# A two-layer encoder in split float32: fourteen more seven-product pairs, weight parts in idle task pages, a new arrangement of the block sums

## The chip, the cores and the metric

The kernel runs on one core of a Trainium2 chip. The metric is the device time of one execution in microseconds. Three runs of the kernel before gave 2572.28, 2573.15 and 2574.47 us; the median is 2573.15 us. The engines are TensorE (PE, with its weight loads shown apart as PEld), VectorE (DVE), ScalarE (ACT), GpSimd (POOL) and SyncE (SP).

## The reference

Two layers over 256 rows of width 4096. Each layer normalises the rows, multiplies by a 4096 x 11264 matrix, runs grouped-query attention and a two-way retention on the parts, gates both, and multiplies by a 4096 x 4096 matrix. All is float32.

```python
for l in range(DEPTH):
    h = rmsnorm(x, norm_w[l])
    proj = h @ w_in[l]                                   # 4096 -> 11264
    aq, ak, av, ag, rq, rk, rv, rg = jnp.split(proj, SPLIT_POINTS, axis=-1)
    aq = apply_axial_rope(rmsnorm(aq), rope) * attn_scale
    ak = apply_axial_rope(rmsnorm(ak), rope)
    a_out = jax.nn.silu(ag) * gqa_attention(aq, ak, av)
    r = bidirectional_retention(rope(rq), rope(rk) * ret_scale, rv, log_gf, log_gb)
    r_out = jax.nn.silu(rg) * rmsnorm(r, ret_norm[l])
    x = x + jnp.concatenate([a_out, r_out], axis=-1) @ w_out[l]   # 4096 -> 4096
return rmsnorm(x, final_norm)
```

## The kernel before

**Products.** The time goes to the two projections. A float32 operand is held as two parts, a high one (rounded to the type fp32r by a copy on ACT) and a low one (the rest, by a subtraction on DVE), and one product is three matmuls of 128x512: high by high, high by low, low by high. The work is cut into 30 blocks of 1024 output columns: phase 0 and 2 (the input projections of the layers) have 11 blocks each, phase 1 and 3 (the output projections) 4 each. A block is written (phase, block), as (1, 2). A block sums over 16 pairs of 256 rows of the inner dimension. A pair is a 2x2 by 2x2 product of submatrices. An "eight" does it with eight products; a "seven" does it with seven products of sums of submatrices (Strassen), so it needs three matmuls fewer, but ready-made sums of the activations (`x7h`, `x7l`: seven forms) and sums of the weights (`wsum`), which DVE makes. Even pairs are always sevens, odd pairs eights, whose activations (`x8h`, `x8l`) hold six forms. The table `MORE` turns an odd pair into a seven in some blocks; `add_forms` then makes the lacking forms from the eight's ones and keeps them in the tile `more` (lines 2000 to 2030).

**Weights.** The weights of an eight come as two raw pages of 128x1024 (kinds A and B). Each gets a high part (`whi`, ACT) and a low part (`wlo`, DVE); a "far" page gets its low part from ACT and a DMA that adds the raw weights to it (`fhi`, `flo`). A seven has four pages: A (raw), T and U (the sums `wsum`, one of 1024 elements and two halves of 512, the second made from the first), and B, of which half is used (`whb`, `wlb`, 512). The buffers: 6 raws, 4 highs, 3 lows, 2 sums, 2 fars, 1 half. Class `Slots` (line 581) counts them.

**Sums of a block.** Each block fills seven PSUM banks M1 to M7. When a bank is done, `combining` (line 1801) adds it to the result tiles `ca` and `cb` on DVE; the next block can only start in a bank that has been read. M5 is added twice, once to each half of `cb`.

**Other work.** Tasks (attention, retention, rotary, gates, residuals) run beside the projections and use 8 task pages of 128x1024 (`PAGES`).

**What sets the order.** The order on every engine is written out while the program is built: clocks of the engines and of the DMA queues are kept in Python, and at each step the engine whose clock is earliest takes the most urgent piece that its model says is ready (`pick`, line 966). `WAYS` gives knobs by block: how early high parts ("high"), sums ("sums") and activations ("split") are made, when tasks may come first ("rush"), and how far ahead of the next block's need the M sums are due ("wait"). On the chip each engine then goes through its list in that order and waits at semaphores; PE too, whose list mixes the products of the tasks into those of the block.

Of the kernel before, what the change touches and what calls it, by code (L numbers as in the profile page):

```python
# [52 lines left out]
WAY = {"rush": 2.8, "split": 6.0, "high": 3.2, "sums": (2.0, 1.99, 1.98), "wait": None}  # L53
WAYS = {
    (0, 1): {"rush": 4.2, "split": 6.0, "high": 3.2, "sums": (2.0, 1.99, 1.98), "wait": 0},
    (0, 2): {"rush": 2.8, "split": 6.0, "high": 3.2, "sums": (2.0, 0.5, 0.4), "wait": None},
    (0, 3): {"rush": 2.4, "split": 6.0, "high": 3.2, "sums": (2.0, 1.99, 1.98), "wait": 0.5},
    (0, 4): {"rush": 2.4, "split": 6.0, "high": 3.2, "sums": (2.0, 1.99, 1.98), "wait": 1},
    (0, 5): {"rush": 2.8, "split": 6.0, "high": 3.2, "sums": (2.0, 1.99, 1.98), "wait": 1},
    (0, 10): {"rush": 2.8, "split": 6.0, "high": 4.5, "sums": (2.0, 1.99, 1.98), "wait": None},  # L60
    (1, 0): {"rush": 2.8, "split": 6.0, "high": 3.2, "sums": (2.0, 1.99, 1.98), "wait": 1},
    (2, 3): {"rush": 4.2, "split": 6.0, "high": 3.2, "sums": (2.0, 1.99, 1.98), "wait": None},
    (2, 4): {"rush": 2.0, "split": 6.0, "high": 3.2, "sums": (2.0, 1.99, 1.98), "wait": 1},
    (2, 5): {"rush": 2.8, "split": 6.0, "high": 3.2, "sums": (2.0, 1.99, 1.98), "wait": 1},
    (2, 10): {"rush": 2.8, "split": 6.0, "high": 4.5, "sums": (2.0, 1.99, 1.98), "wait": None},
    (3, 0): {"rush": 2.8, "split": 6.0, "high": 3.2, "sums": (2.0, 1.99, 1.98), "wait": 1},
# [60 lines left out]
def constants():  # L127
# [27 lines left out]
A11, A12, S4, A22N, S1, S2, S3 = range(7)  # L155
TWO_FORMS = {A11: 0, A12: 2, S3: 4}
# [2066 lines left out]
```

## Time and profile before

| | |
|---|---|
| median of three runs | 2573.15 us |
| the profiled execution | 2574.22 us |
| its span, first to last instruction | 2572.4 us |
| PE busy | 2552.3 us (99%), 11393 matmuls |
| DVE busy | 2405.6 us (94%), 3100 instructions |
| ACT busy | 1954.7 us (76%) |
| mean granted PE clock | 0.998 of full speed |

Busy times are unions: a row of 1.22 us may overlap the next. A matmul's row lasts longer than the distance to the next one, since they are pipelined.

### The profile page before, as it was taken

How to read it: one execution, taken by the hardware profiler on the slowest of the kernel's cores; microseconds unless marked ns; L12 is line 12 of the kernel's file. 1: busy time of each engine (PE TensorE's matmuls, PEld its weight loads, DVE VectorE, ACT ScalarE, POOL GpSimd, SP SyncE). 2: the span in 40 equal slices, each digit the busy share in tenths (PEclk: the TensorE clock that was granted, in tenths of full speed). 3: DMA queues.
4: the chain of work that ended last, by engine and by line, in shares of the span. 5: the costliest groups of instructions: out<-in, count | busy, mean ns of one | idle time of the engine just before them, and what ended most of it. 6: DMA issues, size and time to landing. Idle time of an engine off the chain costs nothing.

```text
span 2572.4 us, 34567 instructions
## 1 busy us (share of the span) xinstructions
PE 2552.3 (99%) x11393; PEld 2099.4 (82%) x11393; DVE 2405.6 (94%) x3100; ACT 1954.7 (76%) x2797; POOL 453.1 (18%) x591
## 2 busy tenths in 40 slices
PE   9999999999999999999999999999999999999998
PEld 5888888888888888788888888887888888888886
DVE  7999999999999999999999999999999989999887
ACT  8877777787777788767887776877887777787675
POOL 0012121221222120112111212211212221201010
PEclk9999999999999999999999999999999999999999
DMA  8989999998998998999999999989999998989897
GB/s 309 311 263 318 269 280 293 281 309 270 277 286 278 284 272 239 277 300 301 304 301 280 292 279 287 283 282 282 296 277 278 276 293 264 283 242 284 252 281 238
DMA packets 212533, 724.91 MB, mean 282 GB/s; under 512 B 25456, under 2 KB 32240, under 8 KB 212352
## 3 DMA queue, kind: packets, MB, share of 16 engines
q1 hardware_dynamic: 147616, 521.31, 57.4%
q0 software_dynamic: 64736, 201.40, 33.8%
q8 instruction: 89, 1.46, 0.2%
q14 instruction: 92, 0.75, 0.1%
HBM read 674.37 MB, written 48.23 MB: 281 GB/s over the span
## 4 chain that ended last, share of the span: by engine, by line
PE 92%; DVE 4%; issue 1%; DMA 1%; POOL 0%; ACT 0%; DVEq 0%; POOLq 0%; ACTq 0%
PE M L1280 89%; PE ps L1280 3%; DVE wlo L315 2%; DVE wsum L315 1%; DVE cb L315 1%; DVE ca L315 0%; DMA flo<-in_w_in 0%; POOL rst L574 0%; DMA nw<-in_norm_wT 0%; PE ps L1115 0%; DVE wlb L315 0%; DVE x8l L315 0%; DVE x7l L315 0%; DVE xf L315 0%; ACT whi L315 0%
## 5 line engine op out<-in xcount | busy, mean ns | idle before, releaser
L315 DVE TENSOR_TENSOR wlo<-wsum,whi 128x1024 fp32r<-128x1024 f32 x486 | 592.2, 1219 | 70.2 <-PE M L1280 54.5
L315 ACT CAST whi<-wsum 128x1024 fp32r<-128x1024 f32 x486 | 509.6, 1049 | 185.9 <-PE M L1280 93.9
L315 DVE TENSOR_TENSOR wlo<-wraw,whi 128x1024 fp32r<-128x1024 f32 x499 | 604.7, 1214 | 6.1 <-ACT whi L315 2.4
L315 ACT CAST whi<-wraw 128x1024 fp32r<-128x1024 f32 x499 | 514.7, 1044 | 94.0 <-PE M L1280 44.2
L1280 PE MATMUL M<-whi,x7h 128*128 128x512 f32 x1428 | 557.1, 390 | 0.3 <-DVE cb L315 0.3
L1280 PE MATMUL M<-whi,x7l 128*128 128x512 f32 x1428 | 555.9, 389 | 0.0
L1280 PE MATMUL M<-wlo,x7h 128*128 128x512 f32 x1428 | 442.7, 391 | 3.0 <-DVE wlo L315 2.8
L1280 PE MATMUL M<-whi,x8h 128*128 128x512 f32 x1026 | 400.1, 390 | 0.5 <-DVE ca L315 0.5
L1280 PE MATMUL M<-whi,x8l 128*128 128x512 f32 x1026 | 399.5, 389 | 0.0
L1280 PE MATMUL M<-fhi,x8h 128*128 128x512 f32 x832 | 324.0, 389 | 0.0
L1280 PE MATMUL M<-fhi,x8l 128*128 128x512 f32 x832 | 323.9, 389 | 0.0
L439 POOL DMA_DIRECT2D flo<-in_w_in x153 | 136.0, 889 | 1029.9 <-ACT flo L315 907.9
L1280 PEld LDWEIGHTS M<-wlo,x7h 128*128 128x128 f32 x1428 | 265.8, 188 | 61.6 <-DVE wlo L315 8.2
L1280 PEld LDWEIGHTS M<-whi,x7h 128*128 128x128 f32 x1428 | 268.2, 188 | 56.7 <-DVE cb L315 1.2
L1280 PEld LDWEIGHTS M<-whi,x7l 128*128 128x128 f32 x1428 | 268.2, 188 | 55.8 <-issue 0.5
L315 DVE TENSOR_TENSOR wsum<-wraw 128x1024 f32<-128x1024 f32 x243 | 296.0, 1218 | 7.7 <-DMA wraw<-in_w_in 3.8
L1280 PE MATMUL M<-wlo,x8h 128*128 128x512 f32 x1026 | 302.1, 390 | 0.4 <-DVE wlo L315 0.4
L315 ACT CAST fhi<-wraw 128x1024 fp32r<-128x1024 f32 (+1 forms) x210 | 218.8, 1042 | 107.0 <-PE M L1280 63.4
L1280 PE MATMUL M<-flo,x8h 128*128 128x512 f32 x832 | 228.4, 389 | 0.0
L1280 PEld LDWEIGHTS M<-whi,x8h 128*128 128x128 f32 x1026 | 192.6, 188 | 42.3 <-DVE ca L315 2.1
L1280 PEld LDWEIGHTS M<-wlo,x8h 128*128 128x128 f32 x1026 | 192.2, 188 | 41.9 <-DVE wlo L315 2.0
L315 ACT ACTIVATE flo<-fhi 128x1024 fp32r<-128x1024 f32 (+1 forms) x210 | 221.3, 1054 | 6.5
(268 smaller groups left out, 3527.3 us busy)
## 6 DMA issues: line engine op xcount, KB each, us to landing
wraw<-in_w_in SPq DMA_DIRECT2D x703, 512.0 KB, 5.9
wraw<-in_w_out SPq DMA_DIRECT2D x256, 512.0 KB, 6.0
flo<-in_w_in POOLq DMA_DIRECT2D x153, 512.0 KB, 8.6
flo<-in_w_out POOLq DMA_DIRECT2D x53, 512.0 KB, 8.5
full<-next_dram POOLq DMA_DIRECT2D x18, 512.0 KB, 9.8
p_dram<-room POOLq DMA_DIRECT2D x64, 128.0 KB, 5.1
pT<-p_dram POOLq DMA_DIRECT2D x16, 512.0 KB, 8.4
next_dram<-room POOLq DMA_DIRECT2D x40, 128.0 KB, 4.8
```

What stands on the lines that cost most here:

```text
L315: return call(out, *args, **kwargs)
L439: getattr(nc, name).dma_start(to, src, **kw)
L1280: nc.tensor.matmul(out, a, b, start=start, stop=stop)
```

## The change

The table `MORE` now names 14 pairs in 11 blocks instead of 5 pairs in 4 blocks. A list `groups_of` spreads the eights between the sevens. The fourth form is A22 instead of its negative, so that an eight's forms hold it already; `add_forms` makes three forms instead of four. The sums of a split, the rotary products, the query splits and the addition of M5 are done in one wide instruction each. `Slots` may take an idle task page for a high part, a low part or a weight sum (`lendable`), by knobs of the block. The knobs of all blocks are new, the order in which the last banks are finished is M3, M4, M5, M2, and `FARS` lists the far pages of nine blocks. The input tables, the first block's direct products, the final block's order and its tail are not in the diff.

```diff
-LAST_ORDER = ("M3", "M5", "M4", "M2")
+LAST_ORDER = ("M3", "M4", "M5", "M2")
-A11, A12, S4, A22N, S1, S2, S3 = range(7)
+A11, A12, A22, S4, S2, S1, S3, A21, D1 = range(9)
+FORMS = {"x7": (A11, A12, A22, S4, S2, S1, S3), "x8": (A11, A12, A21, A22, S3, D1)}
-NINE = ((0, 1), (2, 3), (4,), (6, 5), (7,), (8, 9), (10, 11), (12, 13), (14, 15))
-TEN = ((0, 1), (2,), (4, 3), (6,), (7, 5), (8,), (10, 9), (12,), (13, 11), (14, 15))
-MORE = {(1, 1): NINE, (1, 2): TEN,(3, 1): NINE, (3, 2): NINE}
+MORE = {
+    (0, 1): (9,), (0, 6): (13,), (0, 7): (11,),
+    (1, 1): (3, 11), (1, 2): (5, 13),
+    (2, 1): (5,), (2, 2): (7,), (2, 6): (7,), (2, 7): (5,),
+    (3, 1): (5, 13), (3, 2): (7,),
+}
-    (0, 3): {"rush": 2.4, "split": 6.0, "high": 3.2, "sums": (2.0, 1.99, 1.98), "wait": 0.5},
+    (0, 3): {"sums": (1.5, 0, -0.1), "lend": 1},
...
+    def lendable(n):
+        first = next((v for v in tasks if not v.begun and v.start()), None)
+        need = 0 if first is None else first.need - first.own + (0 if first.own else wanted[0])
+        need = max(need, 2 if to_border() < now_way("stop") else 0)
+        return held[0] + n + pledged() + need + spare() < PAGES and all(v() for v in idle[:n])
     class Slots:
         def ready(self):
-            return self.free and min(self.free) <= now.t
+            return (self.free and min(self.free) <= now.t) or (self.knob is not None and self.lent < now_way(self.knob) and lendable(self.pages))
...
+        def place_of(self, lent, name, n, dt):
+            if lent:
+                return sp.tile([P, 2, NB], dt, tag="pg", name=name, bufs=PAGES)
+            return t(wp, [P, 2, NB], name, n, dt)
...
         def end_u(self, g):
-            ve.tensor_sub(u[:, 1, :], u[:, 0, :], b[:, 1, :])
+            ve.tensor_sub(u[:, 1, :], b[:, 1, :], u[:, 0, :])
...
     def split_pair(p, v, phase, gains, across):
-            ve.tensor_sub(s1, a22n, x1[:, 0])
-            ve.tensor_sub(s3, x0[:, 0], x1[:, 0])
+            ve.tensor_sub(s13, s13, x1[:, 0:1].to_broadcast([P, 2, P // BLK, BLK]))
...
     def rotary(v, L, kind, to):
-            for h in range(2):
-                ve.tensor_mul(dsts[:, :, :, h, :], src[:, :, :, 1 - h, :], ...)
-            ve.tensor_mul(v4[:, m], v4[:, m], C[:, m, :].unsqueeze(1).to_broadcast([P, 4, HD]))
+        ve.tensor_mul(dst, src[:, :, :, :, ::-1, :], S.rearrange(...).unsqueeze(2).to_broadcast(wide))
+        ve.tensor_mul(v4, v4, C.unsqueeze(2).to_broadcast([P, MT, 4, HD]))
...
     def combining(acc, fin, c, order, pages=True):
-        ve.tensor_add(ca[:, 1, :], cb[:, 0, :], acc["M7"])
+        ve.tensor_add(cb[:, 1, :], cb[:, 0, :], acc["M7"])
             if b == "M5":
-                ve.tensor_add(cb[:, 1, :], ca[:, 1, :], acc["M5"])
-                ve.tensor_add(cb[:, 0, :], cb[:, 0, :], acc["M5"])
+                ve.tensor_add(cb, cb, acc["M5"].unsqueeze(1).to_broadcast([P, MT, NB]))
...
     def add_forms(p, phase):
-        ac.copy(parts[:, 0, 0], f[:, 4])
-        ac.copy(parts[:, 0, 2:4], f[:, 5:7])
-        ve.tensor_sub(parts[:, 1, 0], f[:, 4], f32(parts[:, 0, 0]))
-        ve.tensor_sub(parts[:, 1, 2:4], f[:, 5:7], f32(parts[:, 0, 2:4]))
+        ac.copy(parts[:, 0], f[:, 4:7])
+        ve.tensor_sub(parts[:, 1], f[:, 4:7], f32(parts[:, 0]))
```

**Place one: PE in block (0, 1), page A of pair 9.** The numbers tell tiles apart: `x8h_305` is pair 9's activations before, `x8h_315` after. Before, the page is an eight:

```order
L1280 MATMUL M3_978<-whi_1309,x8h_305 128x512
L1280 MATMUL M3_978<-whi_1309,x8l_306 128x512
L1280 MATMUL M5_994<-whi_1309,x8h_305 128x512
L1280 MATMUL M5_994<-whi_1309,x8l_306 128x512
L1280 MATMUL M4_999<-whi_1309,x8h_305 128x512
L1280 MATMUL M4_999<-whi_1309,x8l_306 128x512
L1280 MATMUL M2_1006<-whi_1309,x8h_305 128x512
L1280 MATMUL M2_1006<-whi_1309,x8l_306 128x512
L1280 MATMUL M3_978<-wlo_1345,x8h_305 128x512
L1280 MATMUL M5_994<-wlo_1345,x8h_305 128x512
L1280 MATMUL M4_999<-wlo_1345,x8h_305 128x512
L1280 MATMUL M2_1006<-wlo_1345,x8h_305 128x512
```

After, it is a seven's page A, with a form from `more`:

```order
L1378 MATMUL M1_964<-whi_1309,x8h_315 128x512
L1378 MATMUL M1_964<-whi_1309,x8l_316 128x512
L1378 MATMUL M3_970<-whi_1309,more_961 128x512 x2
L1378 MATMUL M1_964<-wlo_1321,x8h_315 128x512
L1378 MATMUL M3_970<-wlo_1321,more_961 128x512
```

Twelve matmuls into four banks have become six into two ("x2" is two rows that read alike); the seven's pages T, B and U follow further on, in all 21 matmuls against 24.

**Place two: DVE at the end of block (0, 3), where the banks are added to `ca` and `cb`.** Before:

```order
L315 TENSOR_TENSOR cb_3212<-ca_3211,M6_2580 128x512
L315 TENSOR_TENSOR wsum_3257<-wraw_3133,wsum_3241 128x512
L315 TENSOR_TENSOR ca_3211<-cb_3212,M7_2532 128x512
L315 TENSOR_TENSOR wsum_3257<-wsum_3257,wraw_3178 128x512
L315 TENSOR_TENSOR cb_3212<-cb_3212,M3_2488 128x512
L315 TENSOR_TENSOR cb_3212<-ca_3211,M5_2504 128x512
L315 TENSOR_TENSOR cb_3212<-cb_3212,M5_2504 128x512
L315 TENSOR_TENSOR wlo_3285<-wraw_3133,whi_3229 128x1024
L315 TENSOR_TENSOR ca_3211<-ca_3211,M4_2507 128x512
L315 TENSOR_TENSOR wlo_3309<-wraw_3190,whi_3249 128x1024
L315 TENSOR_TENSOR ca_3211<-ca_3211,M2_2512 128x512
```

After:

```order
L358 TENSOR_TENSOR cb_3189<-ca_3188,M6_2562 128x512
L358 TENSOR_TENSOR cb_3189<-cb_3189,M7_2524 128x512
L358 TENSOR_TENSOR cb_3189<-cb_3189,M3_2485 128x512
L358 TENSOR_TENSOR pTl_3227<-pT_3116,pTh_3226 128x1024
L358 TENSOR_TENSOR ca_3188<-cb_3189,M4_2504 128x512
L358 TENSOR_TENSOR cb_3189<-cb_3189,M5_2499 128x1024
L358 TENSOR_TENSOR wsum_3265<-wraw_3123,wsum_3214 128x512
L358 TENSOR_TENSOR wlo_3271<-wraw_3123,whi_3206 128x1024
L358 TENSOR_TENSOR sgT_3114<-ps_3255,sgT_3114 128x2x8x32
L358 TENSOR_TENSOR wsum_3265<-wraw_3152,wsum_3265 128x512
L358 TENSOR_TENSOR ca_3188<-ca_3188,M2_2509 128x512
```

M5's two additions of 512 are one of 1024 and come behind M4's; a low part of an attention task (`pTl`) and the product with the gate (`sgT`) now stand among them. The first `wlo` is the seventh row behind M6's in both; two of the six rows between are of 1024 elements after, none before.

**Place three: DVE in block (1, 1), where the added forms of the block's sevens are made.** Before, one set (pair 7), with two low parts at its end:

```order
L315 TENSOR_TENSOR forms_9872<-x8h_9082,x8l_9083 128x256 x2
L315 SCALAR_TENSOR_TENSOR forms_9872<-forms_9872 128x128
L315 TENSOR_TENSOR forms_9872<-forms_9872 128x128 x2
L315 TENSOR_TENSOR wlb_10064<-wraw_9913,whb_10054 128x512
L315 TENSOR_TENSOR wlo_10070<-wsum_10025,whi_10058 128x1024
L315 TENSOR_TENSOR wlo_10080<-wraw_9969,whi_10066 128x1024
L315 TENSOR_TENSOR wsum_10090<-wraw_9969,wsum_10039 128x512
L315 TENSOR_TENSOR wlo_10097<-wraw_9994,whi_10082 128x1024
L315 TENSOR_TENSOR wsum_10090<-wsum_10090,wraw_9976 128x512
L315 TENSOR_TENSOR wlo_10113<-wsum_10039,whi_10092 128x1024
L315 TENSOR_TENSOR more_9871<-forms_9872,more_9871 128x128
L315 TENSOR_TENSOR more_9871<-forms_9872,more_9871 128x256
```

After, the first of the two sets that the block now holds (pairs 3 and 11):

```order
L358 TENSOR_TENSOR forms_9851<-x8h_8840,x8l_8841 128x256 x2
L358 SCALAR_TENSOR_TENSOR forms_9851<-forms_9851 128x128
L358 TENSOR_TENSOR forms_9851<-forms_9851 128x128 x2
L358 TENSOR_TENSOR wlo_9981<-wsum_9927,whi_9950 128x1024
L358 TENSOR_TENSOR wlo_9989<-wraw_9869,whi_9960 128x1024
L358 TENSOR_TENSOR more_9850<-forms_9851,more_9850 128x384
L358 TENSOR_TENSOR wsum_9999<-wraw_9869,wsum_9954 128x512
L358 TENSOR_TENSOR wlo_10005<-wraw_9888,whi_9973 128x1024
```

The low parts of a set are one instruction of 384 elements; a second set, of the same instructions, stands 33 rows further down, ahead of the addition of the block's M6.

## Rows read from the trace of the kernel before

**Rows 1.** The page: span, and busy time, share and instructions of each engine.

```profile
span 2572.4 us, 34567 instructions
...
PE 2552.3 (99%) x11393; PEld 2099.4 (82%) x11393; DVE 2405.6 (94%) x3100; ACT 1954.7 (76%) x2797; POOL 453.1 (18%) x591
```

**Rows 2.** Windows: busy time (and instructions) of each engine, PE clock, DMA share, GB/s.

```profile
core 0: us, PE busy (x) PEld busy (x) DVE busy (x) ACT busy (x) POOL busy (x), PEclk, DMA share, GB/s
0.00:100.00 100.00, 96.51 (x352) 66.11 (x353) 86.17 (x149) 81.71 (x150) 5.21 (x10) 0.98 0.90 305
100.00:2500.00 2400.00, 2394.99 (x10776) 1983.52 (x10775) 2261.96 (x2876) 1830.62 (x2580) 439.06 (x570) 1.00 0.92 282
2500.00:2573.00 73.00, 60.77 (x268) 49.76 (x266) 57.44 (x77) 42.33 (x69) 8.87 (x11) 0.94 0.75 242
```

**Rows 3.** Waits of PE: what waited for what, us in total, times, longest.

```profile
PE M L1280 <- DVE wlo L315: 3.2, 10, 0.5
PE M L1280 <- ACT full L315: 1.9, 1, 1.9
PE ps L2160 <- DVE whi L2157: 1.5, 1, 1.5
PE ps L1280 <- DVE pTl L315: 0.8, 1, 0.8
```

**Rows 4.** Chain of waits, one unbroken run of matmuls: start, us, what.

```profile
710.37 48.30 PE M L1280 x213
```

**Rows 5.** Timeline of PE at 349: start, us, instruction [idle before <- releaser].

```profile
348.83 0.39 PE L1280 MATMUL M<-whi,x7l 128*128 128x512 f32 x1
349.74 0.73 PE L1280 MATMUL M<-wlo,x7h 128*128 128x512 f32 x2 [0.52 <-DVE wlo L315]
```

**Rows 6.** Timeline of PE at 1791, among the products of an attention task.

```profile
1790.36 0.40 PE L1280 MATMUL ps<-pTh,kv 128*128 128x512 f32 x1
1791.55 0.51 PE L1280 MATMUL ps<-pTl,kv 128*128 128x512 f32 x1 [0.80 <-DVE pTl L315]
```

**Rows 7.** Lines of DVE by form: count | busy us, mean ns | idle before.

```profile
L315 DVE TENSOR_TENSOR wlo<-wraw,whi 128x1024 fp32r<-128x1024 f32 x495 | 601.9, 1218 | 6.1 <-ACT whi L315 2.4 <-issue 1.1 <-ACT xf L315 0.9
L315 DVE TENSOR_TENSOR wlo<-wsum,whi 128x1024 fp32r<-128x1024 f32 x486 | 592.2, 1219 | 70.2 <-PE M L1280 54.5 <-ACT whi L315 13.2 <-ACT whb L315 1.4
L315 DVE TENSOR_TENSOR wsum<-wraw 128x1024 f32<-128x1024 f32 x243 | 296.0, 1218 | 7.7 <-DMA wraw<-in_w_in 3.8 <-DMA wraw<-in_w_out 2.7
...
L315 DVE TENSOR_TENSOR wsum<-wraw,wsum 128x512 f32<-128x512 f32 x243 | 166.2, 684 | 0.4
L315 DVE TENSOR_TENSOR wlb<-wraw,whb 128x512 fp32r<-128x512 f32 x243 | 165.5, 681 | 35.6 <-ACT whb L315 35.6
...
L315 DVE TENSOR_TENSOR cb<-ca,M 128x512 f32<-128x512 f32 x59 | 40.2, 681 | 2.7 <-PE M L1280 1.7 <-ACT ca L315 0.9
...
L315 DVE TENSOR_TENSOR x8l<-full,x8h 128x256 fp32r<-128x256 f32 x78 | 30.4, 418 | 0.7 <-ACT x8h L315 0.4
...
L315 DVE TENSOR_TENSOR xf<-xf,full 128x128 f32<-128x128 f32 x26 | 7.4, 284 | 0.0
```

**Rows 8.** Timeline of DVE, saturated, at 1045.

```profile
1045.95 1.22 DVE L315 TENSOR_TENSOR wlo<-wraw,whi 128x1024 fp32r<-128x1024 f32 x1
1047.09 1.22 DVE L315 TENSOR_TENSOR wlo<-wsum,whi 128x1024 fp32r<-128x1024 f32 x1
```

**Rows 9.** Windows of 100 us, columns as in rows 2.

```profile
300.00:400.00 100.00, 99.26 (x439) 81.53 (x438) 98.44 (x121) 75.02 (x103) 24.20 (x33) 1.00 0.95 293
...
1000.00:1100.00 100.00, 99.14 (x440) 80.90 (x438) 98.23 (x134) 75.94 (x105) 13.74 (x17) 1.00 0.89 267
1100.00:1200.00 100.00, 100.00 (x443) 82.78 (x442) 94.32 (x109) 70.19 (x87) 18.55 (x26) 1.00 0.94 292
1200.00:1300.00 100.00, 99.63 (x439) 81.92 (x438) 97.95 (x136) 82.95 (x126) 19.47 (x26) 1.00 0.99 313
```

**Rows 10.** Waits of ACT from 300 us on.

```profile
ACT whi L315 <- DMA wraw<-in_w_in: 29.9, 20, 3.3
```

More of the change, by code (lines that the diff above doesn't have):

```diff
@@ L476, in drop @@
         own(-n)
+        idle.extend([Ready(now, max(c.done for c in clocks.values()))] * n)
     leaving = []
@@ L627, in __init__ @@
-            self.raws, self.highs, self.sums, self.fars = Slots(RAWS), Slots(HIGHS), Slots(SUMS), Slots(FAR)
-            self.lows, self.halves = Slots(LOWS), Slots(HALVES)
+                    self.start[phase, b] = at
+                    first, last = self.ends(phase, b)
+                    for p, k, use, part in units_in_order(phase, b, first, last, FINAL_ORDER if last else LAST_ORDER, True)[0]:
+                        if part != "D":
+                            self.due.setdefault((phase, p), at)
+                        at += {"D": MM4, "H": 2 * MM[NB], "L": MM[NB]}[part]
@@ L629, in __init__ @@
+            self.raws, self.highs, self.sums, self.fars = Slots(RAWS), Slots(HIGHS, "lend"), Slots(SUMS, "lend"), Slots(FAR, "far", 2)
+            self.lows, self.halves = Slots(LOWS, "lend"), Slots(HALVES)
             self.holds = {"x7": Slots(0), "x8": Slots(0)}
             self.todo, self.ops = [], {"V": [], "A": [], "F": []}
-            at = {}
-            for g in self.pages:
+            self.at, self.adds, self.landed = 0, [], {}
+            self.fresh = None
+            self.plan(self.start)
@@ new lines, in ends, with pages_of @@
+        def ends(self, phase, b):
+            return (phase, b) == (0, 0), (phase, b) == (2 * DEPTH - 1, N_OUT2 - 1)
+        def pages_of(self, phase, b):
+            w = w_out if phase % 2 else w_in
+            first, last = self.ends(phase, b)
+            dues, when = {}, self.start[phase, b]
+            for p, k, use, part in units_in_order(phase, b, first, last, FINAL_ORDER if last else LAST_ORDER)[0]:
+                dues.setdefault((p, k), when)
+                self.bank_due.setdefault((phase, b, use[0]), when)
+                when += {"D": MM4, "H": 2 * MM[NB], "L": MM[NB]}[part]
+            for n, (p, k, uses) in enumerate(pages_in_order(phase, b, first, last)):
+                g = Page()
+                g.pair, g.kind, g.phase, g.block, g.uses = p, k, phase, b, uses
+                g.direct = first and p in DIRECT
+                g.seven = p in sevens(phase, b) and not g.direct
+                g.far = not (g.seven or g.direct) and p in (fars(phase, b) if k == PAGE_B else BOTH_FAR.get((phase, b), ())) and not (first and n < 20)
+                g.held = (PAGE_A, PAGE_B).index(k) if last and p in LATE else None
+                g.at, g.high_at, g.low_at = dues[p, k], None, None
+                g.src = w[phase // 2, b, p]
+                yield g
@@ L779, in low @@
             else:
[L780 to L781 removed]
+                lo, g.low_lent = self.room(self.lows, "wlo", LOWS, F32R)
+                g.lo = self.pieces(g, lo, "l")
             for hi, lo, v in self.each(g, src):
@@ L1026, in hybrid_encoder @@
     version = [-1] * NP
-    phase_now, need_at, border = [-1], {}, {}
-    for g in weights.pages:
-        border.setdefault((g.phase, g.block), g.at)
-        if not g.direct:
-            need_at.setdefault((g.phase, g.pair), g.at)
+    need_at, border = {}, {}
+    border.update(weights.start)
+    need_at.update(weights.due)
     borders_at = sorted(border.values())
@@ L1782, in block @@
                 done.append(p)
-                if p in added and (phase, nb + 1) not in need_more.get(p, ()):
+                if p in added and p not in more(phase, nb + 1):
                     del added[p]
                     drop_after(Ready(now, pe.until + PE_PASS))
-                if last and p not in MIXED and p < NP - 1:
-                    weights.holds["x7" if g.seven else "x8"].give(pe.until + PE_PASS)
+                if last and p < NP - 1:
+                    weights.holds[tag_of(p)].give(pe.until + PE_PASS)
                 if part == "D":
```

286 lines of the change are left out of this document (155 added, 131 removed), and 9 rows, old and new, of the table FARS.

## The prediction

> **What bounds the kernel now.** I read the page first: PE is busy 99% of the span, DVE 94%, ACT 76% [rows 1]. Then the windows, for where PE is not busy: 3.5 us in the first 100, 5.0 us between 100 and 2500, 11.7 us after 2500 (2572.4 less 2500 is 72.4, of which 60.8 are busy) [rows 2]. The first piece is the start (no operand there yet, 1.5 and 1.9 us [rows 3]), the last is the tail, in which the rows are normalised after the last matmul. The change touches neither. So the kernel is the number of matmuls times their distance, and what a change can win is fewer matmuls, or a part of the waits in the middle.
>
> The distance: an unbroken run of 213 matmuls takes 48.30 us [rows 4], 0.2268 us each, at the full clock (1.00 in [rows 2]).
>
> The waits in the middle: PE's list of waits names DVE's low parts, ten waits, 3.2 us, and once 0.8 us for the low part of an attention task [rows 3]. The idle column understates them, since a matmul's row is longer than the distance: at 349 two matmuls start 0.91 us apart instead of 0.23, a loss of 0.68 where the column says 0.52 [rows 5]; at 1791 1.19 us apart, a loss of 0.96 where it says 0.80 [rows 6]. The matmul behind such a place is longer too (0.51 instead of 0.40 in [rows 6]). So I put the waits of the middle between the 5.0 us shown and twice as much, and use 8. They are what DVE does to PE, and where: of the four windows in rows 9, PE idles 0.74, 0.86 and 0.37 us in those with DVE at 98% and nothing in the one at 94% [rows 9]. DVE has no room left there.
>
> **The change part by part.** *Fewer matmuls.* Fourteen added sevens against five, nine more; each takes 21 matmuls in place of 24 (place one: 12 have become 6 on page A, the other pages give 3 back). Counted on the whole PE list it is 27 fewer, all of 128x512: 27 x 0.2268 = **6.1 us off PE**. Nothing hides it, PE being the path.
>
> By the Trainium skill (TensorE: Matmul & The Clock Gate, Back-to-back issue gap) matmuls of 512 columns follow one another at N/2.4 + 2.5 ns, 216 ns; the sum by it would be 5.8 us. The row shows 227 ns [rows 4], and the measurement decides.
>
> *More work for DVE.* A page B that was an eight's is gone with each converted pair, and sums come. From the two lists: 9 more wsum of 1024, 18 more of 512, 9 more wlb, 18 more wlo from sums, 10 fewer wlo from raws. At the rows' 1.218, 0.684, 0.681, 1.219 and 1.218 us [rows 7]: 11.0 + 12.3 + 6.1 + 21.9 - 12.2 = +39.1 us. Added forms: 14 sets in place of 3 (two of the three served two blocks each, none does now). A set is two subtractions or sums of 256 elements (0.418), three of 128 (0.284) and now one of 384, which no row shows; between the rows of 256 and 512, 0.42 and 0.68, I take 0.55. That is 2.24 us x 14 = 31.3, against 3 x 2.4 = 7.2: +24.1 us (23 to 26 with the ends).
>
> *Wide instructions.* No row shows M5 added to both halves from a broadcast bank, nor a rotary product that reads reversed halves. Ends: the plain row of 1024 (1.22 us) and the narrow pieces in a row (2 x 0.681 or 4 x 0.418), that is no gain. I take 1.22, the row of the same size. Then: M5, 29 x (1.36 - 1.22) = 4.1; rotary, 72 of 256 and 36 of 512 become 36 of 1024, 54.8 - 43.9 = 10.9; operand and query splits, 96 of 256 become 48 of 512, 40.1 - 32.8 = 7.3; 64 of 128 in the forms of sevens become 32 of 256, 18.2 - 13.4 = 4.8. Together -27 us (0 with the other end).
>
> The rows of 256 and 512 elements, 418 and 684 ns, leave a fixed part of 152 ns, and 512 elements from PSUM take the same 681 [rows 7]; 181 instructions fewer by 0.15 us are the 27 us again. The Trainium skill (VectorE: DVE Perf Modes, The TRN2 errata) has a table by which the fixed part is 58 cycles of 0.96 GHz from SBUF and 120 from PSUM, 60 and 125 ns; the merges would save 13 us by it, and DVE would gain 50 us of work instead of 36. The same section quotes a measured 151 cycles for this operation in float32, and the trace agrees with that one.
>
> DVE in sum: +39 + 24 - 27 = +36 us. A row overlaps the next by about 0.08 us (rows of 1.22 start 1.14 apart [rows 8]), and there are 74 fewer instructions, so the distance it needs grows by 36 + 6 = 42 us: its 167 us of free time (2572.4 - 2405.6) fall to about 120. ACT gets some 28 us more (18 high parts of sums, 9 halves, copies for the split), with 600 free; no PE wait names its weight parts. DMA issues are the same to one far page.
>
> *Where DVE's work falls.* I priced each block's list, from the addition of one M6 to that of the next, with the rows less 0.083 us. Over the chip's saturated stretch (300 to 400 us [rows 9]) this pricing gives 97.9 us for 100, so 98% of PE's time is what DVE can do. Before, no block past the first asks for more. After, nine do: (1, 0), (1, 1) and (1, 2) together 246.4 us against 244.2 us of PE (232.9 against 244.8 before); (3, 0) and (3, 1) 164.2 against 163.8; (2, 1) and (2, 2) 160.8 against 162.0; (0, 2) 81.6 against 81.7; (2, 6) 81.3 against 82.4. What is short of 98%: 7.1, 3.7, 2.0, 1.5 and 0.5 us, 14.8 in sum. Place three shows how: two sets of forms and two more pairs' sums among the same low parts. Against this stands DVE's lead: three low parts and two sums lie ready, each worth some six matmuls of 0.227 us, 4 us or more in all. Each stretch but the first follows a block with 2 to 11 us to spare, so the lead is full when it begins; the first one overdraws it by about 3 us. That is **+3 us** (0 to 15).
>
> *Task pages.* In the order 70 of about 2480 high parts, low parts and sums lie in a task page: 34, 14 and 22. Where one is taken the lead is a part longer, up to 1.4 us; where its page is still being stored, the writing engine waits, as ACT does for a raw page, 1.5 us each [rows 10], and all its list behind it: the high and low parts that PE wants next, up to 4 us of which the lead covers. Ends: -8 us (all of today's waits gone) and +15 (ten such waits, 1.5 us each, where there is no lead). I take 0, nearest to PE's list, in which no wait of PE is for a page [rows 3].
>
> *New order.* The waits of the middle belong to single places. At 349, the end of (0, 3), DVE adds the banks of seven while PE waits for a `wlo` (place two). Afterwards that `wlo` still stands seventh behind M6, and behind two rows of 1024, so it may be later, 5.3 us after M6 instead of 4.2; but the block has 2.5 us less DVE work, and the knobs set other due times. At 1791 an attention product waited for `pTl` [rows 6]; its place has moved. About 8 us of such waits are dealt anew, with DVE 2% fuller: I count -3: the two places shown cost 0.7 and 1.0 us, and I take nearly as much again for the smaller waits beside them; ends -8 and +5.
>
> *The sum.* -6.1 + 3 + 0 - 3 = -6.1 us. The profiled execution took 2574.22 us, 1.8 us over its span, and would take 2568.1. The median of the runs is 2573.15, 1.07 less: **2567.0 us**.
>
> **The rivals.** 0.2%, 5.1 us, is about what a measurement can tell from no change: faster is below 2568.0, slower above 2578.3.
>
> *A. As forecast*, waits within 2 us of before: 2565 to 2569, of which three quarters lie below 2568.0. For it: the matmuls are certain, and the lists wait on PE in few places. Chance 0.40.
>
> *B. The waits of the middle go.* Earlier sums, loans and 27 us saved by wide instructions fill the lead before each border: 2 to 6 us less, 2561 to 2565. For it: no PE wait for `wlo` is over 0.5 us [rows 3], so a lead one part (1.4 us) longer removes them. Against: DVE has less time, not more. Chance 0.27.
>
> *C. DVE's shortfall shows in the output projections.* The lead is spent in (1, 0) and not refilled before (1, 3); 2 to 11 us more waits: 2569 to 2578, no change. For it: 1000 to 1100 us is a window with DVE full already [rows 9]. Chance 0.22.
>
> *D. DVE becomes the bound.* All of the 14.8 us short reaches PE, because the task lists put attention pieces ahead of `wlo` and no lead stands at the start of the stretches: 2573.15 - 6.1 + 14.8 = 2581.9, slower. It decides from 11.3 us of new waits on. It speaks for it that nine blocks ask for more than 98%, and against it that four of the five stretches are short by under 4 us. Chance 0.11.
>
> **How the numbers follow.** Faster 0.30 of A and all of B: 0.57. Same 0.10 of A and C: 0.32. Slower is D: 0.11. The range is to leave out 2 in 10: from 2562 (the lower part of B out) to 2576 (the upper fifth of C and D out).
>
> **What will show it.** PE's matmuls must fall by 27 and its busy time by about 6 us; DVE's busy time rise by 36 to 42 us. The idle time of PE between 100 and 2500 us must stay near 5 us; if B holds it is under 3, if C or D over 8, and the waits for `wlo` and for bank additions then lie between 930 and 1180 and between 2200 and 2370 us. M5's wide row should read 1.22 us; 1.36 would take 4 us of DVE's room. The forecast is wrong if PE waits for ACT parts or DMA pages, which it does not do now, or if the start or the tail moves.

## The result, and the profile after

The changed kernel takes **2586.5 us** (median of 5 runs, 2582.1 to 2589.6); the kernel before took 2574.5 beside it. The ratio is 1.005, with an interval of 1.0038 to 1.0061: slower by 12.0 us (some 10 to 16 by the interval), where 2567.0 was forecast. The profiled execution took 2589.6 us, 3 us over the median, 1.9 over its span.

The page after, the same two lines as in [rows 1]:

```profile
span 2587.7 us, 34486 instructions
...
PE 2557.3 (99%) x11366; PEld 2092.2 (81%) x11366; DVE 2444.3 (94%) x3026; ACT 1971.8 (76%) x2834; POOL 446.8 (17%) x592
```

27 matmuls fewer, 74 instructions of DVE fewer and 38.7 us more of its work, as worked out ahead. So what was counted came, and the loss is all waiting. One sign looks otherwise: PE's busy time was to fall by about 6 us and rose by 5.0 (2552.3 to 2557.3). A matmul's row is longer behind a wait [rows 6], so some 11 us of the new waits (5.0 + 6.1) stand in PE's busy time and not in its idle time. The windows that answer [rows 2] say where:

```profile
0.00:100.00 100.00, 95.12 (x351) 65.32 (x352) 83.94 (x129) 82.48 (x155) 4.33 (x9) 1.00 0.89 299
100.00:2500.00 2400.00, 2386.95 (x10688) 1965.52 (x10687) 2293.18 (x2811) 1837.14 (x2600) 430.91 (x569) 1.00 0.92 280
2500.00:2590.00 90.00, 75.26 (x330) 61.35 (x328) 67.17 (x87) 52.15 (x81) 11.52 (x14) 0.96 0.80 251
```

Between 100 and 2500 us PE is idle 13.05 us instead of 5.01. The waits of PE, against [rows 3]:

```profile
PE M L1378 <- DVE wlo L358: 7.6, 12, 1.3
PE ps L1204 <- DVE cb L358: 1.8, 2, 0.9
...
PE M L1378 <- DVE cb L358: 1.5, 2, 1.2
PE ps L1378 <- DVE aq L358: 1.2, 4, 0.5
PE M L1378 <- ACT whb L358: 1.1, 1, 1.1
PE M L1378 <- DVE wlb L358: 0.8, 2, 0.5
```

All of the waits shown but one are for DVE, and `wlo` has more than doubled. Idle columns understate, as the prediction said, so the comparisons below use **stalls**: for each two neighbouring matmuls the distance from start to start, less the median distance of that kind (the same tiles and shape), summed over a stretch of the one profiled execution. Before, they come to 14.2 us, after to 36.2. By blocks, of which (1, 0) is 950 to 1036 us after the change, with the runs that are told of further down (us):

```
                (0,0) (0,1)-(0,10) (1,0) (1,1)-(1,3) (2,*) (3,0) (3,1)-(3,3)  all
before           3.2      3.2       0.7      1.6      3.1   0.7      1.7     14.2
after            2.2      7.7       5.7      5.1      4.6   0.5     10.4     36.2
light            2.0      4.4       4.6      2.4      0.7   0.5      3.3     17.8
before_light     1.3      4.5       0.7      1.6      1.1   0.7      1.7     11.6
quick_lo         1.2      1.7       2.9      1.0      0.4   0.1      0.7      8.1
before_quick     1.0      2.0       0.1      0.4      0.8   0.1      0.5      5.0
quick_out        2.5      9.7       4.4      3.1      5.1   0.1      1.9     26.8
after_fat        2.8     12.2       6.3      7.7      8.0   1.6      8.2     46.8
before_fat       2.2      7.6       1.3      3.0      3.3   1.3      3.0     21.7
no_last          2.4      9.4       5.8      6.1      4.4   0.5      3.7     32.3
gate_narrow      2.3      8.8       2.9      6.2      5.0   0.1      5.6     30.9
old_more         2.2      6.8       7.6      2.3      2.7   3.4      2.8     27.7
old_more_light   2.1      7.5       6.8      0.8      2.2   4.8      2.7     26.8
in_more          2.3      8.2       5.8      1.6     17.6  10.9      2.1     48.5
no_out           2.0      9.5       5.5      2.5     12.9   0.5      2.5     35.4
```

Each row is one execution, and the changed kernel's is its slowest of five. quick_out and no_last do what the changed kernel does up to (1, 0), and have 9.7 and 9.4 us in (0, 1)-(0, 10) where it has 7.7: two us in a column are within what a repeat shows.

Of the 22 us of new stalls 17 lie in the output projections. The largest single place lies in the first of their blocks, (1, 0), some 60 us after its start. PE there:

```profile
1011.45 0.39 PE L1378 MATMUL M<-whi,x7l 128*128 128x512 f32 x1
1012.72 0.30 PE L1204 MATMUL ps<-one,cb 128*128 128x128 f32 x1 [0.88 <-DVE cb L358]
1013.96 0.55 PE L1204 MATMUL ps<-one,cb 128*128 128x128 f32 x3 [0.94 <-DVE cb L358]
1015.70 1.22 PE L1378 MATMUL M<-wlo,x7h 128*128 128x512 f32 x2 [1.19 <-DVE wlo L358]
1016.72 0.63 PE L1378 MATMUL M<-whi,x7h 128*128 128x512 f32 x1
1017.14 0.63 PE L1378 MATMUL M<-whi,x7l 128*128 128x512 f32 x1
```

and DVE in the same microseconds:

```profile
1010.03 1.22 DVE L358 TENSOR_TENSOR wsum<-wraw 128x1024 f32<-128x1024 f32 x1
1011.17 0.68 DVE L358 SCALAR_TENSOR_TENSOR cb<-tanh,cb 128x512 f32<-128x512 f32 x1
1011.88 0.69 DVE L358 TENSOR_TENSOR cb<-cb,o 128x512 f32<-128x512 f32 x1
1012.50 0.68 DVE L358 SCALAR_TENSOR_TENSOR cb<-tanh,cb 128x512 f32<-128x512 f32 x1
1013.21 0.69 DVE L358 TENSOR_TENSOR cb<-cb,o 128x512 f32<-128x512 f32 x1
1013.82 0.68 DVE L358 TENSOR_TENSOR wsum<-wraw,wsum 128x512 f32<-128x512 f32 x1
1014.42 1.22 DVE L358 TENSOR_TENSOR wlo<-wsum,whi 128x1024 fp32r<-128x1024 f32 x1
```

DVE has no gap: PE's transposes and then its next low part wait for whatever DVE has not come to. The four gate instructions stand ahead of the low part in DVE's list, and the transposes stand ahead of other matmuls in PE's, so nothing can be taken forward.

In other places DVE is itself held. Its waits for weight loads were 3.8 and 2.7 us before [rows 7]; after:

```profile
DVE wsum L358 <- DMA wraw<-in_w_out: 12.1, 6, 3.4
DVE wsum L358 <- DMA wraw<-in_w_in: 8.4, 8, 1.9
```

6.5 us have become 20.5. The longest in the timeline of DVE after, in block (3, 2), ahead of its stalls:

```profile
2444.66 0.69 DVE L358 TENSOR_TENSOR wlb<-wraw,whb 128x512 fp32r<-128x512 f32 x1
2448.80 1.22 DVE L358 TENSOR_TENSOR wsum<-wraw 128x1024 f32<-128x1024 f32 x1 [3.45 <-DMA wraw<-in_w_out]
```

The chain of waits shows the same from its end (start, us, what). The last long piece of it before, and after, where it could be followed back to 2470 us:

```profile
2317.67 227.47 PE M L1280 x1001
```

```profile
2469.83 15.27 PE M L1378 x66
2488.66 9.49 DMA wraw<-in_w_out
2511.88 11.71 DMA wraw<-in_w_out
2527.07 9.96 DMA wraw<-in_w_out
2543.08 5.40 DMA wraw<-in_w_out
```

An unbroken run of 1001 matmuls, as in [rows 4], has become a chain in which four weight loads alone take 36.6 us. That is the length of the chain and not the loss: PE's stalls from 2470 us on come to about 4 us.

Theory 1 was therefore that DVE has no slack left for the added sevens; its rivals were the new order (theory 2), the borrowed pages (theory 3) and, from the rows just shown, late loads (theory L).

### The profile page after: what moved, and what is told of

The parts are those of the page before. It is cut to its first block, busy times and chain, and to the rows that moved or that the text cites. A ratio compares the mean times of both kernels' runs of the same rounds, so it can differ in the third digit from the quotient of the medians.

```text
span 2587.7 us, 34486 instructions
## 1 busy us (share of the span) xinstructions
PE 2557.3 (99%) x11366; PEld 2092.2 (81%) x11366; DVE 2444.3 (94%) x3026; ACT 1971.8 (76%) x2834; POOL 446.8 (17%) x592
## 5 line engine op out<-in xcount | busy, mean ns | idle before, releaser
L358 ACT CAST whi<-wsum 128x1024 fp32r<-128x1024 f32 x504 | 528.4, 1048 | 219.7 <-DVE wsum L358 166.2
L358 DVE TENSOR_TENSOR wlo<-wsum,whi 128x1024 fp32r<-128x1024 f32 x504 | 613.0, 1217 | 37.7 <-PE M L1378 26.9
L358 DVE TENSOR_TENSOR wlo<-wraw,whi 128x1024 fp32r<-128x1024 f32 (+1 forms) x489 | 591.6, 1212 | 5.4 <-ACT whi L358 3.1
L358 ACT CAST whi<-wraw 128x1024 fp32r<-128x1024 f32 (+1 forms) x489 | 503.0, 1044 | 97.0 <-DMA wraw<-in_w_in 44.7
L1378 PE MATMUL M<-whi,x8h 128*128 128x512 f32 x982 | 383.4, 390 | 0.6 <-DVE cb L358 0.3
L1378 PE MATMUL M<-whi,x8l 128*128 128x512 f32 x982 | 382.5, 389 | 0.0
L358 DVE TENSOR_TENSOR wsum<-wraw,wsum 128x512 f32<-128x512 f32 x504 | 344.1, 683 | 1.2
L358 DVE TENSOR_TENSOR wsum<-wraw 128x1024 f32<-128x1024 f32 x252 | 306.6, 1217 | 21.4 <-DMA wraw<-in_w_out 12.1
L1378 PEld LDWEIGHTS M<-wlo,x7h 128*128 128x128 f32 x1428 | 266.2, 188 | 67.2 <-DVE wlo L358 13.3
L1378 PE MATMUL M<-wlo,x8h 128*128 128x512 f32 x982 | 290.2, 392 | 3.2 <-DVE wlo L358 2.8
L1378 PEld LDWEIGHTS M<-wlo,x8h 128*128 128x128 f32 x982 | 183.1, 188 | 46.9 <-DVE wlo L358 9.9
```

Of the source, the lines that this page charges most:

```text
L358: return call(out, *args, **kwargs)
L1378: nc.tensor.matmul(out, a, b, start=start, stop=stop)
```

## Experiments

Each time is a median, and each ratio is to the kernel before, run on the same chip beside it (2573.5 to 2574.8 us).

### Taking work off DVE: quick_lo, before_quick, quick_out

```diff
-    ve.tensor_sub(lo, v, f32(hi))              # low parts of sums
+    nc.vector.tensor_scalar_mul(lo, f32(hi), 0.0001)
```

The planner still charges the old instruction, so every list stays as it was. quick_out does it in the two output projections alone.

> The changed kernel, every instruction in its place on every engine, but each of the 504 low parts of sums on VectorE is a scaled copy of the high part (tensor by a constant, one source in place of two), so the low parts hold other numbers than the reference needs; it still waits for the same high part. By the rows of one-source instructions (481 ns at 512 columns, 285 at 256) it should take some 0.87 us in place of 1.217: about 7 us less VectorE work for each block of some 82 us. Theory 1 (VectorE overfull): stalls fall by at least the 21 us that were added, time 2560 to 2567 us. Theory 2 (order, bank order): PE still waits where an instruction stands too late in a list or for ACT and DMA; the time falls by 5 us at most, 2581 us or more. Theory 3 (lent task pages make parts wait for their last readers): the waits for pages are PE's and ACT's doing and stay, 2578 us or more.

> The kernel before with the same relief: each low part of a sum on VectorE is a scaled copy of the high part, so the low parts hold other numbers than the reference needs, at about 0.35 us less each, all instructions in their places. A control for the relief itself. Theory 1: before, VectorE kept up, and of its 5 us of stalls after the first 100 us few were VectorE's; the time falls by 1 to 5 us, to 2568 to 2573. If the relief helps any kernel as much as the changed one (a gain of 20 us here too), it doesn't tell that the added sevens are what overfilled VectorE. Theory 2 has no gain here either.

> The changed kernel with every instruction in its place, but the low parts of sums scaled copies of the high parts (other numbers than the reference needs) in the two output projections alone. The same in all blocks took 0.697 us in place of 1.217 each and gave 2563.4 us. Theory 1a (VectorE is late because of the work that stands in the output projections): 16 us of the stalls lie there and go, 2567 to 2572 us, with the 4 to 5 us of new stalls of the input projections left. Theory 1b (it arrives late at the output projections, with work carried over from the input blocks): less than 8 us goes, 2578 us or more, and the stalls of (1, 0), which stand at its start, stay.

Measured: quick_lo 2563.4 us (0.9961, 0.9948 to 0.9974), before_quick 2564.7 (0.9965, 0.9953 to 0.9978), quick_out 2576.9 (1.0011, 1.0001 to 1.0020). The instruction in quick_lo, and DVE's waits for loads there:

```profile
L359 DVE TENSOR_SCALAR wlo<-whi 128x1024 fp32r<-128x1024 f32 x504 | 351.5, 697 | 120.7 <-PE M L1384 79.6 <-ACT whi L360 25.3 <-ACT whb L360 4.9
```

```profile
DVE wsum L360 <- DMA wraw<-in_w_in: 14.0, 9, 3.9
DVE wsum L360 <- DMA wraw<-in_w_out: 8.1, 8, 2.0
```

With 0.52 us less per low part the same list loses 28 of its 36.2 us of stalls, and with them the whole loss: the two kernels stand 1.3 us apart, which their runs don't tell from nothing. The 6.1 us of matmuls saved are not to be seen, so some 4.8 us of waits that the change brought stay. Theory 1 expected this of quick_lo; that the kernel before would gain 9 us was more than the 1 to 5 expected, so DVE costs time there too. DVE still waits 22.1 us for loads in quick_lo, as long as in the changed kernel, and it does no harm: with slack DVE catches up. quick_out fell between its two expectations: against the kernel before beside it, it takes away 9.2 us of quick_lo's 22.6. The stalls of (3, 1) to (3, 3) go almost wholly, 10.4 to 1.9; those of (1, 0) only from 5.7 to 4.4. They don't stand at the block's start, as the expectation has it, but some 60 us into it, so lateness brought from the block before doesn't explain them; gate_narrow, below, does.

### Putting work on DVE: before_fat, after_fat

```diff
-    ve.tensor_sub(lo, v, f32(hi))
+    ve.tensor_sub(lo[:, 0, :], v[:, 0, :], f32(hi)[:, 0, :])
+    ve.tensor_sub(lo[:, 1, :], v[:, 1, :], f32(hi)[:, 1, :])
```

> The kernel before with every low part of a sum that VectorE makes in one instruction of 1024 columns made in two of 512, all else in its place: 486 instructions more, at 2 x 0.683 us started some 0.60 us apart in place of one 1.14 us apart, about 0.066 us each, 32 us of VectorE work over the whole, near the 38.7 us that the change adds, with none of its sevens, order or pages. Theory 1 (VectorE's slack is used up): it gets slower by 8 to 20 us, 2582 to 2594 us, with waits for low parts in the output projections. Theory 2 (order): the slack before takes it, 2574 to 2578 us.

> The changed kernel with the low parts of sums made in two instructions each, as was done to the kernel before, where some 33 us more of VectorE's work cost 8 us (2574.1 to 2582.0). What a microsecond of VectorE's work costs in the changed kernel: Theory 1 (its slack is gone): more than there, 15 to 30 us, 2602 to 2617 us. Theory 2 (the order's fixed waits, no want of slack): no more than there, 2590 to 2595 us.

Measured: before_fat 2582.0 us (1.0032, 1.0020 to 1.0044), after_fat 2604.9 (1.0126, 1.0110 to 1.0142). Busy time of DVE rose by 29.3 us before (2405.6 to 2434.9) and 31.9 after (2444.3 to 2476.2), the time by 7.9 and 19.4 (31.4 less 12.0, each against the kernel before beside it): a microsecond of DVE's work costs 0.27 us in the kernel before and 0.61 in the changed one. after_fat lies within what theory 1 said, before_fat at the edge between the two theories. By the first price the 38.7 us that the change adds would cost about 10 us, by the second 24; the stalls grew by 22. So these two runs can't tell whether fullness alone makes the loss.

### Taking bytes off the queues: light, before_light

```diff
-    getattr(nc, name).dma_start(to, src, **kw)
+    # accumulating loads alone: one half
+    getattr(nc, name).dma_start(to[:, 0, :], src[:, 0, :], **kw)
```

> The changed kernel with its accumulating loads (the second addend of each low part that ScalarE makes, 207 of 512 KB, and the residuals) moving one half of their bytes, so that the other half of these sums is left out; every compute instruction in its place. VectorE waits 20.5 us for weight loads in the changed kernel, 6.5 in the one before, and the queues are some 90% busy. Theory L (the loads come late, and VectorE, once late, stays so): with some 50 MB of 725 gone the loads catch up, VectorE's waits for them fall to 7 us or less, and the time falls by 10 us or more, to 2577 us or less. Theory 1 (VectorE's own work is what is late, and the loads only follow, since it frees their buffers): the waits for loads stay above 12 us, and the time falls by 5 us at most, 2581 to 2586 us.

> The kernel before with the same accumulating loads halved (the other half of those sums left out). A control: both theories expect 2570 to 2574 us, since VectorE waits only 6.5 us for loads there. If it falls by as much as the changed kernel does, the loads are not what the change made worse.

Measured: light 2572.2 us (0.9993, 0.9984 to 1.0002), before_light 2571.5 (0.9992, 0.9983 to 1.0002). DVE's waits for loads in light, and its window between 100 and 2500 us:

```profile
DVE wsum L358 <- DMA wraw<-in_w_in: 2.6, 2, 2.1
...
DVE wsum L358 <- DMA wraw<-in_w_out: 1.3, 1, 1.3
```

```profile
100.00:2500.00 2400.00, 2393.63 (x10760) 1981.13 (x10760) 2306.85 (x2826) 1850.19 (x2614) 431.16 (x573) 1.00 0.84 259
```

The expectation of theory L, and against theory 1 in its bare form: DVE does the same work (2444.8 us over the span, 2444.3 in the changed kernel), the DMA engines are busy 0.84 instead of 0.92, and against the kernel before beside it the changed kernel falls by 13.4 us, the one before by 2.0. So in this list both are needed for the loss, loads that come late and a DVE without room to make it good; either cure takes it away. ACT's waits for weight loads fall with DVE's (its high parts `whi` and `fhi`: 106.8 to 32.3 us, and 90.2 to 21.8 in the kernel before), so the run doesn't tell on which of the two engines the late loads do their harm. The four pairs side by side:

```
us against the kernel before       before   changed   the change
as they are                          0       +12.0      +12.0
low parts faster (quick)            -9.3     -10.6       -1.3
loads lightened (light)             -2.0      -1.4       +0.6
low parts slower (fat)              +7.9     +31.4      +23.5
```

### Fewer sevens: old_more, in_more, no_out, no_last

```diff
 MORE = {                     # old_more: the five of before
-    (0, 1): (9,), ... (3, 2): (7,),
+    (1, 1): (7,), (1, 2): (7, 13), (3, 1): (7,), (3, 2): (7,),
 # in_more: the seven of the input projections and these five
 # no_out: the seven of the input projections alone
 # no_last: all fourteen without (3, 1) and (3, 2)
```

> The changed kernel with the five added sevens of the kernel before in place of its fourteen; policies, lent pages, wide sums and the bank order stay. Nine sevens fewer are 27 more matmuls of 0.2268 us: +6.1 us of PE work. Theory 1 (VectorE is overfull: the nine sevens' sums and low parts, mostly for the output projections, make it late, and PE waits): PE's stalls fall from 35.8 us to some 15, and the time to 2586.5 + 6.1 - 21 = about 2572 us. Theory 2 (the new order does it: bank order, policies by block, lent pages, whatever the number of sevens): the stalls stay near 36 us and the time goes up to about 2592 us. Between them, near 2582, both have a share.

> The changed kernel with its seven added sevens of the input projections kept, and the output projections' as in the kernel before (five): twelve in all, two fewer, 6 matmuls more, +1.4 us. Theory 1 by place: 16 of the 21 us of new stalls lie in the eight output blocks and go with the two sevens and their places; the time falls to 2572 to 2575 us. Theory 2: the order and bank order make them, the time stays at 2586 to 2590 us.

> The changed kernel with its seven added sevens of the input projections and none in the output projections: 21 matmuls more, +4.8 us. The order from the first output projection on is made anew. Theory 1: the unforeseen stalls of (1, 2) and (3, 1) to (3, 3) go and those at the entry of (1, 0) stay in part: stalls of some 20 us in place of 35.8, about 2575 to 2577 us. Theory 2: any order that differs from the kernel before's costs its 20 us whatever the number of sevens: 2590 us or more, as with five sevens.

> The changed kernel without the three added sevens of the last output projection, (3, 1) and (3, 2): TensorE's list is the changed kernel's word for word up to the last output projection, and nothing else is undone. Nine more matmuls of 0.2268 us: +2.0 us. So it parts the sevens from the order as the first comparison (2590.6 us with five sevens, where the whole list had been made anew) could not. Theory 1 (VectorE has no slack for the sevens): of the 10.4 us of stalls in (3, 1) to (3, 3) some 8 go: 2586.5 + 2.0 - 8 = about 2580 us. Theory 2 (the order and the policies, not the sevens): the stalls stay, 2588 us or more.

Measured: old_more 2590.6 us (1.0067, 1.0052 to 1.0082), in_more 2603.3 (1.0110, 1.0095 to 1.0125), no_out 2596.3 (1.0094, 1.0075 to 1.0112), no_last 2588.8 (1.0053, 1.0038 to 1.0068). Not one did what theory 1 said, and in the first three theory 2 is nearer. They don't give the price of the sevens, since another table makes the whole list anew, and each new list has waits of its own: (1, 0) costs 5.5 to 7.6 us in all of them; in_more and no_out each wait once long for an accumulated far part, in in_more

```profile
PE M L1366 <- DMA flo<-in_w_in: 4.9, 1, 4.9
```

One thing they do answer, which matters most for the cause. From old_more's page, and DVE's waits for weight loads there:

```profile
PE 2555.6 (99%) x11393; PEld 2101.0 (81%) x11393; DVE 2392.3 (93%) x2912; ACT 1961.6 (76%) x2808; POOL 455.1 (18%) x595
```

```profile
DVE wsum L346 <- DMA wraw<-in_w_in: 22.5, 17, 2.5
DVE wsum L346 <- DMA wraw<-in_w_out: 10.7, 5, 4.4
```

old_more has the five sevens of the kernel before and 13.3 us less work for DVE than that kernel (2392.3 against 2405.6), and yet takes 16.7 us longer, and its DVE waits 33.2 us for loads instead of 6.5. no_out is alike: 2404.8 us of DVE's work, 22.2 us longer, 45.2 us of waits. So in these two lists it is not the added work that brings the loss or the late loads; the list that the new planner writes does.

Only no_last keeps PE's list word for word up to the last output projection. There the stalls of (3, 1) to (3, 3) fall from 10.4 to 3.7 us, near what was expected, for 2.0 us of matmuls. Its time shows no gain: in the identical part before, its profiled execution has 2.9 us more stalls, and the changed kernel's runs already spread over 7.5 us. So these stalls go with the sevens of the last projection and the list made for them; which of the two makes them, and what they cost in time, isn't settled.

### Borrowed pages: lent_named

```diff
-    return sp.tile([P, 2, NB], dt, tag="pg", name=name, bufs=PAGES)
+    return sp.tile([P, 2, NB], dt, tag="pg", name="lent" + name, bufs=PAGES)
```

> The changed kernel, the same instructions, with the 70 weight parts that borrow task pages named so that the profile tells them apart (34 high parts, 14 low, 22 sums). Theory 3 (borrowed pages make parts wait): writers of these parts wait for the pages' last readers, over 5 us in sum, and PE waits behind them. Theory 1 and 2: they wait under 2 us in sum, as the planner lends only pages that are free.

Measured: one run, 2589.6 us. The waits of those who write a borrowed page:

```profile
ACT lentwhi L358 <- DVE wsum L358: 11.7, 8, 2.6
ACT lentwhi L358 <- DMA wraw<-in_w_in: 3.8, 3, 2.1
ACT lentwhi L358 <- DMA wraw<-in_w_out: 1.7, 1, 1.7
...
DVE lentwsum L358 <- DMA wraw<-in_w_out: 1.0, 1, 1.0
```

All are waits for the source of the part, a sum or a load, none for a reader of the page. Theory 3 falls.

### What is left: gate_narrow, old_more_light

```diff
-    ve.scalar_tensor_tensor(acc[:, m, :], e[:, m, :], 1.0, acc[:, m, :], ...)
-    ve.tensor_mul(acc[:, m, :], acc[:, m, :], o[:, m, :])
+    (both on [:, m, :64])
```

> The changed kernel with the two gate instructions of the retention heads (16 instructions of some 0.61 us pitch, four of them just before the stall at 1012 us) done on 64 of 512 columns, so that the rest of the gate is left out; the list is unchanged. If the place of the four gate instructions ahead of a sum and its low part makes the stall of (1, 0), the three waits there, 3.5 us in the changed kernel, fall to under 2 us. If VectorE is simply behind by then, with its backlog from the block before, they stay at 3 us or more. The time moves by 4 us at most either way, 2582 to 2588 us.

> The changed kernel with the old five sevens and with the accumulating loads halved (half of those sums left out). Theory L, late loads on a VectorE without slack, for the order made anew as well: 2590.6 falls by 10 us or more, to 2580 us or less. If the order's own waits make the loss there: 2585 us or more.

Measured: gate_narrow 2584.6 us (1.0039, 1.0025 to 1.0053), old_more_light 2585.1 (1.0041, 1.0026 to 1.0056). With the gate out of the way, PE at the same place in (1, 0):

```profile
1012.44 0.60 PE L1204 MATMUL ps<-one,cb 128*128 128x128 f32 x4
1013.91 0.73 PE L1378 MATMUL M<-wlo,x7h 128*128 128x512 f32 x2 [0.88 <-DVE wlo L358]
```

Of the three waits there one is left, 1.05 us of stall for 3.53 (a later one, 1.1 us for ScalarE's copy of another head, comes in its place), and the block's stalls halve, 5.7 to 2.9: the gate's work at that place in DVE's list makes that stall, an order fixed when the program is built. light says the same: with the loads out of the way the three waits are as long as in the changed kernel, 3.5 us. The 2.2 us in the time, against the kernel before beside it, are within the spread. old_more_light went against theory L: lighter loads halve old_more's waits for loads (33.2 to 15.8 us) but save only 6.3 us, each median against the kernel before beside it; 10.3 us of loss stay. Its two profiled executions are only 0.7 us apart, so their stalls (27.7 and 26.8) don't show the gain. Its largest, 6.8 and 4.8 us in (1, 0) and (3, 0), were 7.6 and 3.4 with the full loads: they are the order's own.

No kernel that does the whole computation came out ahead of the one before.

## Why the prediction was wrong

The account by the runs: -6.1 us for 27 matmuls; with the loads lightened the change still loses 0.6 us, so its list has 0.6 + 6.1 = 6.7 us more waits of its own (by the stalls 17.8 - 11.6 = 6.2); and 12.0 - 0.6 = 11.4 us come from late loads that DVE can't make good. -6.1 + 6.7 + 11.4 = +12.0. The 12.0 is known to some 3 or 4 us, and 11.4 with it. The prediction's sum had +3 and -3 in the places of 11.4 and 6.7.

- *Fewer matmuls, -6.1*: held, 27 fewer, and their distance is 0.227 us (median of all of a kind) as before.
- *More work for DVE, +36 to 42 us*: held, +38.7 (ACT got 17.1 us, where 28 were counted). The two forms that no row had shown, M5 in one instruction and the set of 384:

```profile
L358 DVE TENSOR_TENSOR cb<-cb,M 128x1024 f32<-128x1024 f32 x29 | 35.2, 1214 | 0.8
...
L358 DVE TENSOR_TENSOR more<-forms,more 128x384 fp32r<-128x384 f32 x14 | 7.7, 550 | 3.2 <-ACT more L358 3.2
```

  1.214 us was put at 1.22, and 0.550 at 0.55.
- *Where DVE's work falls, +3 (0 to 15)*: this step failed. It asked whether DVE's instructions fit into a block's time, took 98% as what DVE can do, and let a lead of 4 us cover nearly all that was short. It put nothing on a DVE that stands still for a load: of the loads the prediction says only that their issues are the same to one far page. In the changed kernel 20.5 us of such waits stand in DVE's list, and DVE has no room to catch up. The measure is 11.4 us, within the range given for the step but not at the value taken, and not by its mechanism alone, since old_more has the waits and a loss without the added work. The places named were half right: (1, 0) to (1, 2) took 8.0 us more, of which 3.9 are the order's (next point), and (3, 0) and (3, 1) 2.0; the whole of phase 2, with three of the nine blocks named, only 1.5. (3, 2) and (3, 3), with 6.6, were not named, nor was (0, 1), with 2.5. In (3, 2) and (3, 3) DVE is not even full:

```profile
2394.00:2478.00 84.00, 82.76 (x361) 66.82 (x360) 75.30 (x86) 57.29 (x68) 7.74 (x9) 1.00 0.91 269
2478.00:2558.00 80.00, 77.15 (x337) 62.61 (x336) 69.84 (x80) 54.82 (x76) 11.26 (x13) 1.00 0.89 267
```

  DVE is busy 75.3 of 84 us and 69.8 of 80, 90% and 87%, but 9.2 of its 20.5 us of waits for loads stand there (2.7 in the same blocks before). A sum of instructions by block doesn't show these two.
- *New order, -3 (-8 to +5)*: this step failed too, in its sign: +6.7 by the light pair, outside its ends, and 4.8 by the quick pair, just inside. It looked at two waits that might go, and not at places that had none: (1, 0) alone has 3.9 us of it in light (4.6 against 0.7), where the gate stands ahead of a low part.
- *Task pages, 0*: held; in lent_named no writer of a borrowed page waits for its reader.
- *The rivals*: D named the outcome, 2581.9 us, and nearly the right price, 14.8 us, for 11.4. That is partly luck: its sum has nothing for the new order's 6.7 us, and its reason, DVE as the bound, is half of what was found; light shows that DVE can do all of its work in 2572 us if it is fed. D had 0.11, against it that four of five stretches are short by under 4 us, a sum of instructions again. The list of PE's waits before told that the kernel before kept up, not by how much: what before_quick (9.3 us) and before_fat (0.27 us for each us) show, that DVE already cost time there, stood in no row that was read.
- *What would show it*: PE's idle time over 8 us was named as the sign of C or D, and is 13.05. The longer waits lie in part where they were looked for, from 1012 to 1163 us and at 2317 to 2356, in part behind, at 2467 to 2495 and 2554. One wait for an ACT part of the weights, 1.1 us, came as well. The start and the tail stayed as they were.

Two things stay open. One is why this list waits more for its loads. The loads themselves are no slower: from issue to landing they take 6.0 and 5.8 us (input and output weights, medians) against 5.9 and 6.0 before, and the DMA engines are busy 0.92 in both. SP's queue waits longer for loads of output weights to land, 45.0 us against 18.9, but shorter for input weights, 66.5 against 94.2, in sum no longer. The other is how much of the 11.4 us the nine sevens alone make, since a list without them is another list in every place; old_more and no_out say that a list of this planner can lose as much without the added work.

## What to carry to other kernels

Where an engine is 94% busy and its order is fixed at build time, price a change of its list not by whether the work fits but by what each late input then costs, and look for those inputs (here DVE's own waits for loads) before the change. A run of the old kernel with work added to the engine, and one with work taken from it, gives that price before the change is written. And a list that is made anew has new waits everywhere, even where its work is less (old_more), so an edit that leaves the list as it is, and changes only how long one kind of instruction takes, tells causes apart where removing part of the change can't.

## What the runs showed of the hardware

TensorE's granted clock fell after the three waits at 1012 to 1015 us, in which it did only four small transposes. Windows of the changed kernel, then of gate_narrow, where one wait of 0.88 us is left at that place, and of light, where the three waits are as long (0.87, 0.94 and 1.19 us, the last ending at 1012.1):

```profile
1010.00:1016.00 6.00, 2.99 (x14) 1.94 (x13) 5.93 (x9) 5.97 (x11) 0.00 (x0) 0.94 0.58 163
1016.00:1019.00 3.00, 3.00 (x10) 2.34 (x10) 3.00 (x4) 1.50 (x3) 0.88 (x1) 0.56 0.77 186
1019.00:1022.00 3.00, 3.00 (x17) 2.51 (x16) 2.85 (x7) 2.61 (x4) 0.00 (x0) 1.00 1.04 274
```

```profile
1014.00:1016.00 2.00, 1.91 (x7) 1.15 (x7) 2.00 (x3) 1.97 (x3) 0.00 (x0) 1.00 0.01 4
```

```profile
1012.00:1016.00 4.00, 3.82 (x18) 2.89 (x19) 4.00 (x6) 3.10 (x7) 0.88 (x1) 1.00 0.83 194
```

From 1015.2 to 1018.6 us the granted clock is 0.5, the lower of its two levels, 1.2 GHz (0.56 is the mean of a window that reaches past it), and the matmuls start 0.43 us apart instead of 0.23. Five of them lose 0.2 us each and their neighbours some 0.5 us together, so the waits of 3.5 us cost about 5.0. In light the clock stayed at 1.00 after the same waits: here they came before the fall, but they didn't bring it about each time.

An instruction of DVE with one source tensor of 1024 float32 elements takes 697 ns, one with two sources 1217 [quick_lo's row above, rows 7].
